# Where the split weights start inside their buffers, and a 64-byte shift of cross-attention operands, in a two-layer decoder on one core

## The chip, the core and the metric

The kernel runs on one core of one Trainium2 chip. The metric is device time in microseconds (us), the time from the launch's start to its end on the core. Three runs of the kernel before took 1091.21, 1092.42 and 1090.48 us; the median is 1091.21 us. Nothing runs on the other cores.

## The reference

The reference computes a decoder of two layers over 256 tokens of width 1024, in float32. Each layer adds three things to the residual x, each after an RMSNorm:

```python
for l in range(DEPTH):                       # DEPTH = 2
    h = rmsnorm(x, norm_mix[l])
    x = x + mixer_block(h, ...)              # z = h @ w_in; four token mixers; gates; w_branch; w_out
    x = x + cross_attention(rmsnorm(x, norm_xattn[l]), rmsnorm(mem, norm_mem[l]), wq, wk, wv, wo)
    x = x + squared_relu_mlp(rmsnorm(x, norm_mlp[l]), w_up, w_down)   # relu(h @ w_up)**2 @ w_down
return rmsnorm(x, norm_final)
```

In `mixer_block`, `w_in` has 6840 columns; 4096 of them are gates, the rest feed latent attention (MLA), a spatial gate, gated linear attention and a gated DeltaNet. Cross-attention has 4 heads of 256 over 256 memory tokens: scores are q times k, then a softmax, then its result times v. The hidden width of the MLP is 4096.

## The kernel before

**Two parts.** A float32 weight is not multiplied as it is. ScalarE (ACT) copies it, rounded, into a buffer `wh` of type float32r, and VectorE (DVE) writes the rest, `w - wh`, into `wl`. Activations are split the same way (`xh` and `xl`, `hh` and `hl`, and so on). Each product is then three matmuls, in `mm3`: high by high, high by low, low by high (L202 to L204).

**The stream of weights.** All weights lie in DRAM as a list of halves of [128, 1024] float32, 168 for each layer, in the order of use. `half()` (L178) takes the next one: every second call starts a transfer of 1 MB into one of three buffers `wr`, and each call splits one half into one of four buffers `wh` and one of four `wl`. A half holds eight blocks of 128 columns. In most products a block is the stationary operand (128 columns), and 256 columns of activations (all tokens) are the moving one; the profile writes such a matmul as `128*128 128x256`. In four places (`gemm_tok`) it is the other way round: 128 columns of activations are stationary and 512 columns of weights move.

**The stages of a layer**, in their order, with the number of halves: `z` (18, input columns), `tok` (4, by `gemm_tok`), MLA's two halves, `gate` (32), `k` (8), `br` (8, `w_branch`), `out` (8), `q` (8), `v` (8, by `gemm_tok`), `o` (8), `up` (32), `down` (32; by `gemm_tok` in the second layer). The many small products of the four mixers lie between the products of `gate`; the scheduler of the framework puts them there, by its own model of times. A gate product, a transpose or a sum of squares (L356, one column) that comes between two streamed products is called an interruption below.

**Places.** Each `wh` and `wl` buffer has 512 bytes of slack, and `PLACE` (L49) says for each stage at which byte the half begins, as a list of pairs (for `wh`, for `wl`) that successive halves take in turn: `b, c = (n // 4 for n in Stream.place[...])` (L189), then `wh[:, b : b + 1024]`. In the built program every `wh` and `wl` buffer starts at byte 256 modulo 512 of its partition, and the activations of the products with 256 columns (`xh`, `xl`, `hh`, `hl`, `mh`, `ml`, `ah`, `al`, `oh`, `ol`, `kx`, `qx`, `ph`, `pl`, `vx`, and so on) start at 448 modulo 512. Counted modulo 256, places 0 and 256 are therefore 64 bytes past the activations, places 128 and 384 are 192 bytes past them, and place 448 starts level with them. This text calls them **class A** (0, 256), **class B** (128, 384) and **class C** (448).

Before, by stage (place of `wh`, place of `wl`):

| stage | layer 0 | layer 1 |
|---|---|---|
| z | (0,0), (256,256): A | (256,256), (384,384): A and B by halves |
| gate | (256,256), (384,384): A and B by halves | (0,256): A |
| k | (0,0), (128,128): A and B by halves | (384,384), (0,0): B and A by halves |
| br | (128,128), (384,384): B | (0,0), (256,256): A |
| out, q, o | (256,256): A | (256,256): A |
| up | (256,384): A for `wh`, B for `wl` | (0,0), (256,256): A |
| down | 0, 128, 256, 384 in turn: A and B by halves | (448,448), `gemm_tok` |
| tok, MLA, v | (448,448): C | (448,448): C |

In cross-attention the scores (L1182) have q stationary and k moving, and the products with v (L1213) have v stationary and the softmax `ph`, `pl` moving; all four start at 448 modulo 512, so they are class C too.

Of the kernel before, what the change touches and what calls it, by code (L numbers as in the profile page):

```python
# [9 lines left out]
F32 = mybir.dt.float32  # L10
F32R = mybir.dt.float32r
# [32 lines left out]

SLACK = 512
ONE, TOK = [(256, 256)], [(448, 448)]
PLACE = [  # L49
    dict(z=[(0, 0), (256, 256)], tok=TOK, gate=[(256, 256), (384, 384)], k=[(0, 0), (128, 128)], br=[(128, 128), (384, 384)],  # L50
         out=ONE, q=ONE, v=TOK, o=ONE, up=[(256, 384)], down=[(0, 0), (128, 128), (256, 256), (384, 384)]),
    dict(z=[(256, 256), (384, 384)], tok=TOK, gate=[(0, 256)], k=[(384, 384), (0, 0)], br=[(0, 0), (256, 256)],
         out=ONE, q=ONE, v=TOK, o=ONE, up=[(0, 0), (256, 256)], down=TOK),
]
N_PIECE = 44
# [13 lines left out]
def decoder(ctx: ExitStack, tc: tile.TileContext, ws, xn_d, xt_d, mem_d, pos_d, fin_d, par_d, cst_d, msk_d, out_d):  # L69
# [12 lines left out]
    def nm(s):  # L82
        uid[0] += 1
        return f"{s}_{uid[0]}"
# [43 lines left out]
    xs += [cp.tile([P, 2, T], F32, name=f"x{j}") for j in range(1, 4)]  # L128
    hh, hl = [], []
    cs = cp.tile([P, T], F32, name="cs")  # L130
    rowm = cp.tile([P, T], F32, name="rowm")
# [41 lines left out]
    class Stream:  # L173
        i = 0
        raw = None
        place = PLACE[0]["z"]

    def half(parts=1):  # L178
        if Stream.i % 2 == 0:
            if Stream.i < 4:  # L180
                Stream.raw = raw0[Stream.i // 2]
            else:
                Stream.raw = wp.tile([P, 2048], F32, tag="wr", name=nm("wr"), bufs=3)
                nc.sync.dma_start(Stream.raw, ws[Stream.i // 2])
        o = 1024 * (Stream.i % 2)
        Stream.i += 1
        r = Stream.raw[:, o : o + 1024]
        wh, wl = (wp.tile([P, 1024 + SLACK // 4], F32R, tag=n, name=nm(n), bufs=4) for n in ("wh", "wl"))
        b, c = (n // 4 for n in Stream.place[Stream.i % len(Stream.place)])  # L189
        wh, wl = wh[:, b : b + 1024], wl[:, c : c + 1024]  # L190
        n = 1024 // parts
        for c in range(0, 1024, n):
            p = slice(c, c + n)
# [53 lines left out]
    def ch(tiles):  # L247
        return lambda k: tiles[k // 2][:, k % 2, :]
# [113 lines left out]

    def gate_tile(i, dt=F32, name="gt"):
        return ap.tile([P, 2, T], dt, tag=f"gt{i}", name=nm(name))

# [76 lines left out]
    def layer(l):  # L442
# [17 lines left out]

        def weights(stage):
            Stream.place = PLACE[l][stage]

        weights("z")


# [275 lines left out]
        def zin_rest():  # L742
# [13 lines left out]

            weights("tok")
            gemm_tok(X, XL, 8, ev_tok)

        def head_out(n, o, z, gcol, post, pre, name):  # L760
# [309 lines left out]
        if l == 0:  # L1070
            for j in range(4):
                for d, n in ((hh, "hh"), (hl, "hl")):
                    d.append(ap.tile([P, 2, T], F32R, tag=f"{n}{j}", name=nm(n)))
        for j in range(4):
# [52 lines left out]

        weights("gate")
        for m in range(8):
# [25 lines left out]
        weights("k")  # L1155
        gemm(ch(mh), ch(ml), 8, 4, ev_split(kh, kl, "kx"))

        weights("br")
        for m in range(8):
            merge(m)  # L1160
        rel(brh, brl)
        weights("out")

# [6 lines left out]
        qh, ql = [], []  # L1170
        weights("q")

        gemm(H, L, 8, 4, ev_split(qh, ql, "qx"), lead=True)
        px = [[None] * 2 for _ in range(2)]
        for a in range(2):
            for t in range(2):
# [11 lines left out]
                px[a][t] = p  # L1188
        rel(qh, ql, kh, kl)
        vh, vl = [[None] * 2, [None] * 2], [[None] * 2, [None] * 2]  # L1190
        weights("v")
        for nb in range(2):
            def ev_v(t, ps):
# [3 lines left out]
                vh[t][nb], vl[t][nb] = a, b  # L1197
            gemm_tok(ch(mh), ch(ml), 8, ev_v)
        rel(mh, ml)
        oh, ol = [], []  # L1200
        weights("o")
        for h in range(4):
            ps = bank()
            for mt in range(2):
                for t in range(2):
                    PE.transpose(ps[:, mt, 128 * t : 128 * t + 128], px[h // 2][t][:, h % 2, 128 * mt : 128 * mt + 128], ident)
            ph, pl = new(F32R, name="ph"), new(F32R, name="pl")
            split_ps(ph, pl, ps)
# [7 lines left out]
            oh.append(a), ol.append(b)  # L1216
            rel(ph, pl)
        rel(px, vh, vl)
# [21 lines left out]

        weights("up")
        gemm(H, L, 8, 16, ev_up, lead=True)
        weights("down")
        if l + 1 < NL:
# [6 lines left out]
    def final(rs, ah, al):  # L1251
# [16 lines left out]
        for nb in range(2):  # L1268

            @urgent  # L1270
            def evac(t, ps):
# [12 lines left out]
                S.dma_start(out_d[:, t, 512:1024], u)  # L1284

            gemm_tok(ch(ah), ch(al), 32, evac, 4 if nb else 1)
        rel(y, yg, gf, sq)
# [186 lines left out]
```

## Time and profile before

| | |
|---|---|
| median of three runs | 1091.21 us |
| the profiled execution | 1090.66 us |
| its span, from first to last instruction | 1088.3 us |
| TensorE matmul busy (PE) | 1064.5 us, 98% of the span |
| VectorE busy (DVE) | 812.7 us, 75% |
| ScalarE busy (ACT) | 583.8 us, 54% |
| matmuls in the trace | 8494 |

A matmul's record has a start and a modelled end, some 276 ns later. Matmuls are pipelined: the next one starts 113 to 118 ns after, while the first still runs. So the busy share and the duration say little of the pace; the pace is the distance from start to start. It is read here in two ways: in a list of instructions in order of time, from the column of starts, and in a table of stretches, from the count of matmuls in a stretch of known length.

### The profile page before, as it was taken

To read this page: it belongs to the slowest core of one execution; us is meant where nothing else is said; L and a number is where in the kernel's file an instruction comes from. 1 tells how busy PE (TensorE), PEld (TensorE's weight loads), DVE (VectorE), ACT (ScalarE), POOL (GpSimd) and SP (SyncE) were. 2 spreads that over 40 slices of the span, in tenths; PEclk is the share of its full clock that TensorE was granted. 3 is DMA by queue.
4 is the path that set the end of the run, shared out by engine and by line. 5 is a ranking of instruction groups with operands and counts; after the bars stand their busy time and mean duration, and the time that the engine had idled before them with its cause. 6 is when DMAs were issued, how large, how long until landed. Compare 5 with 4: busy or idle time off the path is not lost.

```text
span 1088.3 us, 20696 instructions
## 1 busy us (share of the span) xinstructions
PE 1064.5 (98%) x8494; PEld 1020.9 (94%) x8494; DVE 812.7 (75%) x1419; ACT 583.8 (54%) x875; POOL 197.6 (18%) x170
## 2 busy tenths in 40 slices
PE   9989999999999999999999999999999999999996
PEld 8979998899998999999999899989999899999885
DVE  7999857789866876655689997686797778665454
ACT  6565554554645666644455746544555555555342
POOL 6334005108300200000102321410451011010000
PEclk9999999999999999999999999999999999999998
DMA  9442523354544455555555343334455345554551
GB/s 364 170 173 107 207 105 122 112 194 156 194 155 155 160 195 195 194 194 194 195 188 202 140 167 141 117 144 152 171 193 194 132 142 192 194 206 165 194 191 39
DMA packets 28319, 185.13 MB, mean 170 GB/s; under 512 B 3392, under 2 KB 3648, under 8 KB 6976
## 3 DMA queue, kind: packets, MB, share of 16 engines
q1 hardware_dynamic: 26208, 179.09, 45.4%
q10 hardware_dynamic: 2016, 4.72, 1.3%
q8 instruction: 66, 1.08, 0.4%
q14 instruction: 29, 0.24, 0.1%
HBM read 182.75 MB, written 1.05 MB: 169 GB/s over the span
## 4 chain that ended last, share of the span: by engine, by line
PE 81%; DVE 11%; ACT 3%; DMA 2%; issue 1%; POOL 1%; ACTq 0%; DVEq 0%; POOLq 0%
PE g L202 24%; PE g L204 24%; PE g L203 24%; DVE wl L198 3%; DMA mr<-memt 2%; DVE qt L865 1%; PE ps L202 1%; ACT wh L195 1%; PE ps L203 1%; PE ps L204 1%; DVE gt L1116 1%; PE ps L666 1%; PE ps L670 1%; DMA wr<-ws 1%; DVE mgl L1124 1%
## 5 line engine op out<-in xcount | busy, mean ns | idle before, releaser
L198 DVE TENSOR_TENSOR wl<-wr,wh 128x1024 fp32r<-128x1024 f32 (+1 forms) x337 | 415.3, 1235 | 182.9 <-ACT wh L195 181.2
L195 ACT ACTIVATE wh<-wr 128x1024 fp32r<-128x1024 f32 (+1 forms) x337 | 355.1, 1057 | 332.9 <-PE g L203 233.8
L204 PE MATMUL g<-hh,wl 128*128 128x256 f32 x1152 | 324.0, 282 | 3.4 <-DVE wl L198 3.4
L202 PE MATMUL g<-hh,wh 128*128 128x256 f32 x1152 | 322.5, 281 | 1.9 <-ACT gt L1101 1.5
L203 PE MATMUL g<-hl,wh 128*128 128x256 f32 x1152 | 321.6, 279 | 0.0
L204 PEld LDWEIGHTS g<-hh,wl 128*128 128x128 f32 x1152 | 216.4, 188 | 5.6 <-DVE wl L198 4.4
L202 PEld LDWEIGHTS g<-hh,wh 128*128 128x128 f32 x1152 | 216.3, 188 | 3.1 <-ACT gt L1101 1.9
L203 PEld LDWEIGHTS g<-hl,wh 128*128 128x128 f32 x1152 | 218.0, 189 | 0.4 <-issue 0.2
L342 POOL TENSOR_TENSOR sq<-sq,sq 128x512 f32<-128x512 f32 x14 | 23.3, 1661 | 341.0 <-ACT sq L334 340.8
L203 PE MATMUL g<-xl,wh 128*128 128x256 f32 x272 | 75.4, 279 | 0.3 <-DVE xl L324 0.3
L202 PE MATMUL g<-xh,wh 128*128 128x256 f32 x272 | 74.8, 279 | 0.6 <-ACT xh L315 0.6
L204 PE MATMUL g<-xh,wl 128*128 128x256 f32 x272 | 74.5, 279 | 0.0
L202 PE MATMUL g<-ah,wh 128*128 128x256 f32 x256 | 70.7, 276 | 0.0
L203 PE MATMUL g<-al,wh 128*128 128x256 f32 x256 | 70.7, 276 | 0.0
L204 PE MATMUL g<-ah,wl 128*128 128x256 f32 x256 | 70.7, 276 | 0.0
L202 PEld LDWEIGHTS g<-xh,wh 128*128 128x128 f32 x272 | 50.8, 188 | 1.3 <-ACT xh L315 1.3
L1117 POOL TENSOR_TENSOR gt<-gt,gt 128x512 f32<-128x512 f32 x16 | 35.5, 2218 | 90.8 <-DVE gt L1116 89.9
L203 PEld LDWEIGHTS g<-xl,wh 128*128 128x128 f32 x272 | 51.1, 188 | 0.5 <-DVE xl L324 0.5
L204 PEld LDWEIGHTS g<-xh,wl 128*128 128x128 f32 x272 | 50.8, 189 | 0.0
L204 PE MATMUL g<-wh,al 128*128 128x512 f32 x128 | 49.5, 389 | 0.0
L203 PE MATMUL g<-wl,ah 128*128 128x512 f32 x128 | 49.5, 389 | 0.0
L202 PE MATMUL g<-wh,ah 128*128 128x512 f32 x128 | 49.4, 390 | 0.0
(500 smaller groups left out, 2331.0 us busy)
## 6 DMA issues: line engine op xcount, KB each, us to landing
wr<-ws SPq DMA_DIRECT2D x166, 1024.0 KB, 4.8
wr<-ws ACTq DMA_DIRECT2D x4, 512.0 KB, 7.5
mr<-memt ACTq DMA_DIRECT2D x8, 256.0 KB, 4.7
par<-par SPq DMA_DIRECT2D x2, 778.0 KB, 6.8
x<-xt SPq DMA_DIRECT2D x3, 256.0 KB, 7.8
cst<-cst SPq DMA_DIRECT2D x1, 588.0 KB, 8.4
gf<-fin SPq DMA_DIRECT2D x2, 256.0 KB, 5.3
yt<-yg ACTq DMA_DIRECT2D x2, 256.0 KB, 2.5
```

The costliest lines, as they stand in the source:

```text
L195: i = S.activation(wh[:, p], r[:, p], AF.Copy)
L198: V.tensor_tensor(wl[:, p], r[:, p], wh[:, p].bitcast(F32), op=ALU.subtract)
L202: PE.matmul(out, ah, bh, start=start, stop=False)
L203: PE.matmul(out, ah, bl, start=False, stop=False)
L204: PE.matmul(out, al, bh, start=False, stop=stop)
L342: G.tensor_tensor(acc, acc, sq, op=ALU.add)
L666: PE.matmul(xp[:, h], M[:, h], Tm[:, h], start=True, stop=True)
L670: PE.matmul(up[:, h], X[t][:, h], U[:, h], start=True, stop=True)
L865: V.tensor_tensor(qt[:, a].rearrange("p (b h) -> p b h", h=h), e3, halves(qbd[a // 2][:, a % 2], i)[:, :, 1], op=ALU.mult)
L1116: V.scalar_tensor_tensor(gt[m][a], gt[m][a], 1.0, ps, op0=ALU.add, op1=ALU.mult)
L1117: G.tensor_tensor(gt[m][0], gt[m][0], gt[m][1], op=ALU.add)
L1124: V.scalar_tensor_tensor(dl, t, 0.5, dh.bitcast(F32), op0=ALU.mult, op1=ALU.subtract)
```

## The change

The list `PLACE` goes. A half no longer lies in one piece: its first four blocks start at byte 256 of the buffer and its last four, shifted, at byte 2432 (`TURN`, in floats: 64 and 608). Modulo 512 of the partition the first four blocks start at 0 and the last four at 128: class A, then class B, in every half, in `wh` and in `wl` alike, in all stages with 256 moving columns and in MLA's two halves. `gemm_tok` keeps the address it had, 448 (`TOK`, in floats 112 and 624, without a gap). `wh` and `wl` are split with one instruction for a half as before; its shape is 2x512 in place of 1024. `Weights` translates a column of a half into its place.

q of cross-attention moves from the pool of general pieces into the tiles that the gates and `xh`, `xl` use, and `ph`, `pl` move into the tiles of `hh` and `hl`. These tiles are widened from 2048 to 2560 bytes, and in them q, `ph` and `pl` start 64 bytes later (`SHIFT`, 16 floats): at 0 modulo 512. k and v stay at 448.

On each of the five engines the instructions of the built program stand in the same order as before.

```diff
-SLACK = 512
-ONE, TOK = [(256, 256)], [(448, 448)]
-PLACE = [
-    dict(z=[(0, 0), (256, 256)], tok=TOK, gate=[(256, 256), (384, 384)], k=[(0, 0), (128, 128)], br=[(128, 128), (384, 384)],
-         out=ONE, q=ONE, v=TOK, o=ONE, up=[(256, 384)], down=[(0, 0), (128, 128), (256, 256), (384, 384)]),
...
-]
+W_BUF = 1152
+TURN, TOK = (64, 608), (112, 624)
+
+SHIFT = 16
...
+    class Weights:
+        def __init__(self, t, place):
+            self.t, self.place = t, place
+        def __getitem__(self, k):
+            c = k[1]
+            o = self.place[c.start // 512] - c.start // 512 * 512
+            return self.t[:, c.start + o : c.stop + o]
+
+    def two(t, place):
+        n = place[1] - place[0]
+        return t[:, place[0] : place[0] + 2 * n].rearrange("p (s c) -> p s c", s=2)[:, :, 0:512]
...
-        wh, wl = (wp.tile([P, 1024 + SLACK // 4], F32R, tag=n, name=nm(n), bufs=4) for n in ("wh", "wl"))
-        b, c = (n // 4 for n in Stream.place[Stream.i % len(Stream.place)])
-        wh, wl = wh[:, b : b + 1024], wl[:, c : c + 1024]
...
-                i = S.activation(wh[:, p], r[:, p], AF.Copy)
+                i = S.activation(hi, ri, AF.Copy)
...
-                V.tensor_tensor(wl[:, p], r[:, p], wh[:, p].bitcast(F32), op=ALU.subtract)
-        return wh, wl
+                V.tensor_tensor(lo, ri, hi.bitcast(F32), op=ALU.subtract)
+        return Weights(wh, Stream.place), Weights(wl, Stream.place)
...
+    def spaced(tag, dt, name, shift=0):
+        t = ap.tile([P, 640], dt, tag=tag, name=nm(name))
+        return t, t[:, shift : shift + 512].rearrange("p (a b) -> p a b", a=2)
...
-                a, b = new(F32R, name=name), new(F32R, name=name)
+                if name == "qx":
+                    a, b = (gate_tile(2 * p + i, F32R, name, SHIFT) for i in range(2))
+                else:
+                    a, b = new(F32R, name=name), new(F32R, name=name)
...
-            ph, pl = new(F32R, name="ph"), new(F32R, name="pl")
+            ph, pl = (hfull[2 * h + i][:, SHIFT : SHIFT + 512].rearrange("p (a b) -> p a b", a=2) for i in range(2))
```

## Rows read from the trace of the kernel before

**Rows 1.** The page: span; busy time and share of each engine; the chain of work that ended last, by engine.

```profile
span 1088.3 us, 20696 instructions
...
PE 1064.5 (98%) x8494; PEld 1020.9 (94%) x8494; DVE 812.7 (75%) x1419; ACT 583.8 (54%) x875; POOL 197.6 (18%) x170
...
PE 81%; DVE 11%; ACT 3%; DMA 2%; issue 1%; POOL 1%; ACTq 0%; DVEq 0%; POOLq 0%
```

**Rows 2.** Table of stretches: `up` of layer 0, `down` of layer 0 and `up` of layer 1, 80 us out of each. Columns: stretch in us from the span's start, its length, busy us and (x) number of instructions of each engine, granted TensorE clock, DMA share, GB/s.

```profile
375.00:455.00 80.00, 80.00 (x708) 80.00 (x707) 57.43 (x74) 49.07 (x61) 0.00 (x0) 1.00 0.54 197
462.00:542.00 80.00, 80.00 (x709) 80.00 (x708) 46.91 (x45) 35.77 (x41) 5.16 (x4) 1.00 0.54 197
906.00:986.00 80.00, 80.00 (x681) 80.00 (x681) 55.29 (x68) 46.95 (x59) 4.01 (x2) 1.00 0.54 196
```

**Rows 3.** The matmuls of TensorE in order of time at the start of `up` in layer 0, around the sum of squares (L356). Columns: start us, us, engine, line, operation, tiles, shapes, count.

```profile
374.81 0.28 PE L204 MATMUL g<-hh,wl 128*128 128x256 f32 x1
374.92 0.50 PE L356 MATMUL ps<-cst,sq 128*128 128x1 f32 x4
375.28 0.48 PE L202 MATMUL g<-hh,wh 128*128 128x256 f32 x2
375.60 0.28 PE L203 MATMUL g<-hl,wh 128*128 128x256 f32 x1
375.72 0.28 PE L204 MATMUL g<-hh,wl 128*128 128x256 f32 x1
375.84 0.28 PE L203 MATMUL g<-hl,wh 128*128 128x256 f32 x1
...
377.31 0.28 PE L204 MATMUL g<-hh,wl 128*128 128x256 f32 x1
```

**Rows 4.** The same list at the start of `up` in layer 1, around the same sum of squares.

```profile
903.98 0.28 PE L204 MATMUL g<-hh,wl 128*128 128x256 f32 x1
904.09 0.50 PE L356 MATMUL ps<-cst,sq 128*128 128x1 f32 x4
904.46 0.48 PE L202 MATMUL g<-hh,wh 128*128 128x256 f32 x2
904.77 0.28 PE L203 MATMUL g<-hl,wh 128*128 128x256 f32 x1
...
906.42 0.28 PE L203 MATMUL g<-hl,wh 128*128 128x256 f32 x1
```

**Rows 5.** The same list in `z` of layer 1: two transposes (L305) while a half of class B is used; the next half, of class A, begins with the row at 559.59.

```profile
558.67 0.38 PE L305 MATMUL ps<-cst,rsmixy 128*128 128x128 f32 x2
558.80 0.36 PE L202 MATMUL g<-xh,wh 128*128 128x256 f32 x1
559.00 0.28 PE L203 MATMUL g<-xl,wh 128*128 128x256 f32 x1
...
559.47 0.28 PE L204 MATMUL g<-xh,wl 128*128 128x256 f32 x1
559.59 0.28 PE L202 MATMUL g<-xh,wh 128*128 128x256 f32 x1
559.70 0.28 PE L203 MATMUL g<-xl,wh 128*128 128x256 f32 x1
559.83 0.28 PE L204 MATMUL g<-xh,wl 128*128 128x256 f32 x1
559.95 0.28 PE L202 MATMUL g<-xh,wh 128*128 128x256 f32 x1
560.06 0.28 PE L203 MATMUL g<-xl,wh 128*128 128x256 f32 x1
...
560.51 0.28 PE L204 MATMUL g<-xh,wl 128*128 128x256 f32 x1
```

**Rows 6.** The same list in `gate` of layer 0: a half of class B after an interruption; the next half, of class A, begins with the row at 145.62.

```profile
144.36 0.36 PE L204 MATMUL g<-hh,wl 128*128 128x256 f32 x1
...
145.62 0.28 PE L202 MATMUL g<-hh,wh 128*128 128x256 f32 x1
...
147.39 0.28 PE L202 MATMUL g<-hh,wh 128*128 128x256 f32 x1
```

**Rows 7.** Table of stretches (columns as in rows 2): `q` of layer 0 and of layer 1; two stretches of `k` in layer 1, before and after a half of class B is followed by one of class A.

```profile
296.00:310.00 14.00, 14.00 (x121) 14.00 (x120) 9.74 (x16) 7.05 (x11) 0.00 (x0) 1.00 0.51 188
825.00:839.00 14.00, 14.00 (x122) 14.00 (x121) 9.74 (x16) 7.05 (x11) 0.00 (x0) 1.00 0.50 191
...
763.00:766.00 3.00, 3.00 (x27) 3.00 (x27) 2.15 (x3) 1.95 (x3) 0.00 (x0) 1.00 0.10 22
...
770.00:773.00 3.00, 3.00 (x29) 3.00 (x29) 2.07 (x3) 1.06 (x1) 0.00 (x0) 1.00 0.52 175
```

**Rows 8.** Table of stretches: the end of `z` in layer 0 and in layer 1, then the whole of `gate` in layer 0 and in layer 1.

```profile
38.00:60.00 22.00, 21.99 (x186) 21.67 (x185) 21.85 (x40) 11.65 (x17) 4.39 (x3) 1.00 0.48 177
...
576.00:596.00 20.00, 20.00 (x173) 20.00 (x173) 20.00 (x32) 10.38 (x14) 4.52 (x3) 1.00 0.58 211
74.00:221.00 147.00, 139.69 (x1200) 133.88 (x1199) 118.07 (x305) 82.83 (x150) 40.54 (x41) 1.00 0.36 130
609.00:751.00 142.00, 139.06 (x1204) 134.02 (x1203) 110.40 (x287) 77.75 (x143) 31.84 (x35) 1.00 0.38 138
```

**Rows 9.** The list of matmuls at the first and the last pair of starts more than 115 ns apart in `gate` of layer 0 (419 of 763 starts).

```profile
75.25 0.28 PE L202 MATMUL g<-hh,wh 128*128 128x256 f32 x1
75.36 0.28 PE L203 MATMUL g<-hl,wh 128*128 128x256 f32 x1
...
220.81 0.28 PE L204 MATMUL g<-hh,wl 128*128 128x256 f32 x1
220.93 0.28 PE L202 MATMUL g<-mh,wh 128*128 128x256 f32 x1
```

**Rows 10.** Table of stretches, TensorE alone (columns: stretch, length, busy us and number of matmuls, granted clock, DMA share, GB/s): scores of cross-attention, and products with v, in layer 0.

```profile
312.70:316.70 4.00, 4.00 (x35) 1.00 0.37 107
347.20:350.20 3.00, 3.00 (x28) 1.00 0.00 0
```

**Rows 11.** Groups of DVE by line and shape, with the mean ns of one: the split of a half; a product of 512 contiguous elements; a product whose second operand is read as 2x256.

```profile
L198 DVE TENSOR_TENSOR wl<-wr,wh 128x1024 fp32r<-128x1024 f32 x335 | 414.0, 1238 | 176.4 <-ACT wh L195 174.7
...
L1237 DVE TENSOR_TENSOR al<-up,ah 128x512 fp32r<-128x512 f32 x32 | 22.1, 692 | 1.8 <-ACT ah L1236 1.7
...
L487 DVE TENSOR_TENSOR zc<-g,rrow 128x512 f32<-128x512 f32 x3 | 2.0, 680 | 0.0
```

More of the change, by code (lines that the diff above doesn't have):

```diff
@@ L43 @@
 PAD = 48
-SLACK = 512
-ONE, TOK = [(256, 256)], [(448, 448)]
-PLACE = [
-    dict(z=[(0, 0), (256, 256)], tok=TOK, gate=[(256, 256), (384, 384)], k=[(0, 0), (128, 128)], br=[(128, 128), (384, 384)],
-         out=ONE, q=ONE, v=TOK, o=ONE, up=[(256, 384)], down=[(0, 0), (128, 128), (256, 256), (384, 384)]),
-    dict(z=[(256, 256), (384, 384)], tok=TOK, gate=[(0, 256)], k=[(384, 384), (0, 0)], br=[(0, 0), (256, 256)],
-         out=ONE, q=ONE, v=TOK, o=ONE, up=[(0, 0), (256, 256)], down=TOK),
-]
+W_BUF = 1152
+TURN, TOK = (64, 608), (112, 624)
+SHIFT = 16
 N_PIECE = 44
@@ L129, in decoder @@
     hh, hl = [], []
+    hfull = []
     cs = cp.tile([P, T], F32, name="cs")
@@ L175, in decoder, with one @@
         raw = None
-        place = PLACE[0]["z"]
+        place = TURN
+    class Weights:
[5 more added lines that the diff above has]
+            return self.t[:, c.start + o : c.stop + o]
+    def one(t, place, c):
+        return t[:, place[c] : place[c] + 512]
+    def two(t, place):
+        n = place[1] - place[0]
+        return t[:, place[0] : place[0] + 2 * n].rearrange("p (s c) -> p s c", s=2)[:, :, 0:512]
     def half(parts=1):
@@ L187, in half @@
         r = Stream.raw[:, o : o + 1024]
-        wh, wl = (wp.tile([P, 1024 + SLACK // 4], F32R, tag=n, name=nm(n), bufs=4) for n in ("wh", "wl"))
-        b, c = (n // 4 for n in Stream.place[Stream.i % len(Stream.place)])
-        wh, wl = wh[:, b : b + 1024], wl[:, c : c + 1024]
-        n = 1024 // parts
-        for c in range(0, 1024, n):
-            p = slice(c, c + n)
+        wh, wl = (wp.tile([P, W_BUF], F32R, tag=n, name=nm(n), bufs=4) for n in ("wh", "wl"))
+        for c in range(parts):
+            ri, hi, lo = (two(t, p) if parts == 1 else one(t, p, c) for t, p in ((r, (0, 512)), (wh, Stream.place), (wl, Stream.place)))
             with tc.high_priority(offset=WP):
-                i = S.activation(wh[:, p], r[:, p], AF.Copy)
+                i = S.activation(hi, ri, AF.Copy)
                 if Stream.i <= 4:
                     tc.keep_in_program_order(i)
-                V.tensor_tensor(wl[:, p], r[:, p], wh[:, p].bitcast(F32), op=ALU.subtract)
-        return wh, wl
+                V.tensor_tensor(lo, ri, hi.bitcast(F32), op=ALU.subtract)
+        return Weights(wh, Stream.place), Weights(wl, Stream.place)
     def mm3(out, ah, al, bh, bl, start, stop):
@@ L361, in gain, with gate_tile @@
         return nrm[:, 8 * i : 8 * i + 8]
-    def gate_tile(i, dt=F32, name="gt"):
-        return ap.tile([P, 2, T], dt, tag=f"gt{i}", name=nm(name))
+    def spaced(tag, dt, name, shift=0):
+        t = ap.tile([P, 640], dt, tag=tag, name=nm(name))
+        return t, t[:, shift : shift + 512].rearrange("p (a b) -> p a b", a=2)
+    def gate_tile(i, dt=F32, name="gt", shift=0):
+        return spaced(f"gt{i}", dt, name, shift)[1]
     def operands(j, g, mix=False, parts=(slice(0, 2),), share=False):
@@ L459, in layer @@
         H, L = ch(hh), ch(hl)
-        def weights(stage):
-            Stream.place = PLACE[l][stage]
-        weights("z")
         zc = []
@@ L755, in ev_tok @@
                 R.zs.append(z)
-            weights("tok")
+            Stream.place = TOK
             gemm_tok(X, XL, 8, ev_tok)
+            Stream.place = TURN
         def head_out(n, o, z, gcol, post, pre, name):
@@ L1072, in layer @@
                 for d, n in ((hh, "hh"), (hl, "hl")):
-                    d.append(ap.tile([P, 2, T], F32R, tag=f"{n}{j}", name=nm(n)))
+                    t, v = spaced(f"{n}{j}", F32R, n)
+                    hfull.append(t), d.append(v)
         for j in range(4):
@@ L1126, in merge @@
                 rel(gt[m])
-        weights("gate")
         for m in range(8):
@@ L1161, in layer @@
         rel(brh, brl)
-        weights("out")
         gemm(ch(mgh), ch(mgl), 8, 4, residual(gain(4 * l + 1)), lead=True, tail=True)
@@ L1170, in layer @@
         qh, ql = [], []
-        weights("q")
         gemm(H, L, 8, 4, ev_split(qh, ql, "qx"), lead=True)
@@ L1188, in layer @@
                 px[a][t] = p
-        rel(qh, ql, kh, kl)
+        rel(kh, kl)
         vh, vl = [[None] * 2, [None] * 2], [[None] * 2, [None] * 2]
-        weights("v")
+        Stream.place = TOK
         for nb in range(2):
@@ L1198, in layer @@
             gemm_tok(ch(mh), ch(ml), 8, ev_v)
+        Stream.place = TURN
         rel(mh, ml)
         oh, ol = [], []
-        weights("o")
         for h in range(4):
@@ L1216, in layer @@
             oh.append(a), ol.append(b)
-            rel(ph, pl)
         rel(px, vh, vl)
@@ L1239, in ev_up @@
             rel(t)
-        weights("up")
         gemm(H, L, 8, 16, ev_up, lead=True)
-        weights("down")
         if l + 1 < NL:
@@ L1284, in evac @@
                 S.dma_start(out_d[:, t, 512:1024], u)
+            Stream.place = TOK
             gemm_tok(ch(ah), ch(al), 32, evac, 4 if nb else 1)
```

2 lines of the change are left out of this document (removed).

## The prediction

> **What bounds the kernel now.** I read the page first. TensorE is busy 98% of the span and carries 81% of the chain that ended last [rows 1], so TensorE's pace sets the end. A busy share near 100% does not show whether that pace is the best one, so the second view is the table of stretches, with a count of matmuls. In `up` of layer 0 and in `down` of layer 0, 80 us hold 708 and 709 matmuls; in `up` of layer 1, which runs the same code with other places, they hold 681 [rows 2]. Nothing waits in any of the three: PE is busy 80.00 of 80.00 us, the granted clock is 1.00, DVE and ACT have 20 us and more to spare. So there are two paces for one and the same matmul. 80 us over 708.5 is 112.9 ns, 80 us over 681 is 117.5 ns; the starts in the list of matmuls agree (375.84 to 377.31 us is 13 steps of 113 ns, 904.77 to 906.42 us is 14 steps of 118 ns) [rows 3, 4]. I call them close and wide; a wide one costs 4.5 ns more. Counted start to start over the whole trace, 2,604 of 6,560 streamed products with 256 columns are wide (116 to 126 ns), 3,955 close.
>
> The third view, the list in order of time, tells how the wide pace begins and ends. Both `up` stages are close until the sum of squares (L356) comes between two products. After it both are wide. In layer 0, where `wh` is in class A and `wl` in class B, the pace is close again from the fourth or fifth product on [rows 3]. In layer 1, where all lies in class A, it stays wide for the 30 halves that follow [rows 2, 4]. So an interruption sets the pace, and the places decide how long it lasts. To the starts I put the addresses of the built program and counted unbroken stretches in which one class is followed by the other while the pace is wide: from B to A it becomes close in 11 of 14 (one of them is close from the fourth product after the turn on [rows 5]), and stays wide in 3 (one of them [rows 6]); from A to B it becomes close in 0 of 9; from A to A (places 0 and 256) in 0 of 35. In 51 turns of either direction with a close pace it stayed close. Class C is always wide, 120 ns and more.
>
> **The change part by part.** *The turn inside each half.* Each half now goes A, B, and the next half begins with A: a turn from B to A after every 24 products in every stage, where before it came after 48 or never. A wide stretch should then last to the next half, or the one after, in place of to the end of its stage. I took each wide stretch of the trace and cut it at the first start of a half, with 8 cures in 10.
>
> - `up` of layer 1: 727 wide of 767, of which 12 are left; 715 x 4.5 ns = 3.2 us. DVE has 25 us of 80 to spare there [rows 2], so all of it reaches the end.
> - `q` in both layers: 152 wide of 192 each (14 us hold 121 and 122, while the close pace gives 126) [rows 2, 7]; some 17 are left: 2 x 135 x 4.5 ns = 1.2 us, passed on whole.
> - `k`: 55 and 109 wide, 48 left: 0.5 us; that a turn from B to A does it there is seen in 27 against 29 matmuls in 3 us [rows 7]. `out` of layer 1: 46 to 22, 0.1 us. `br`: 89 to 68, 0.1 us. MLA's products, class C before, 82 to 46: 0.15 us.
> - `gate`: 419 and 421 wide of 763 each (the first and the last of layer 0 in [rows 9]), cut to 306 and 207: 327 x 4.5 ns = 1.5 us. Here much is between the products and DVE is busy 118 of 147 and 110 of 142 us with the chains of the mixers [rows 8]; the chain goes over DVE for 11% of the span [rows 1]. I let half through: 0.7 us (bounds 0 and 1.5).
> - `z`: 336 wide, cut to 85: 1.1 us. But its wide products lie at its end, and there DVE is busy 21.85 of 22 and 20.00 of 20 us [rows 8]. A faster TensorE would only wait for `wl` (L198). I let 0.2 us through (bounds 0 and 1.1).
>
> `up` and `down` of layer 0 and `o` are close now and should stay so: nothing in 51 turns speaks for a loss. `gemm_tok` keeps its addresses: nothing.
>
> *The 64 bytes.* The scores run at class C: 35 matmuls in 4.00 us [rows 10], the edges taken off (33 steps) 121 ns. With q at 0 and k at 448 they become class A, so 113 to 118 ns; 95 products x 6.5 ns = 0.6 us at best, 0.25 us if they stay wide. For v at 448 stationary and the softmax at 0 moving, the trace has no row: the stationary is there 64 bytes before the moving operand modulo 256, no longer behind it. Its bounds are the level start it has now (28 in 3.00 us, some 115 to 121 ns) [rows 10], so 0, and the close pace, 90 x 7 ns = 0.6 us; a loss as large as the gain cannot be excluded either. I take 0.3 us. For the scores I take 0.6 us.
>
> *The splits.* 335 splits of a half are read and written as 2x512 in place of 1024. A product of DVE with an operand read as 2x256 took 680 ns, one with 512 contiguous elements 692 ns [rows 11]: no cost; at the worst a few ns on 1238, which DVE hides in `up` and which would cost 335 x 10 ns = 3 us only if it were on the chain everywhere, while the chain lies on DVE for 11%: 0.4 us. The order of instructions does not change on any engine, nor do SP's transfers; the widened tiles change addresses of other tiles by multiples of 512 only.
>
> *Sum.* 3.2 + 1.2 + 0.5 + 0.1 + 0.1 + 0.15 + 0.7 + 0.2 + 0.6 + 0.3 = 7.05, rounded 7 us. The profiled execution took 1090.66 us (span 1088.3 [rows 1] and 2.4 us around it), so it would be 1083.7; the median of the runs is 0.55 us above it, so the time is about 1084.2, said as 1084. The floor, all 2,604 close at once with both parts of cross-attention, is 2,604 x 4.5 ns + 1.2 = 12.9 us less: 1078.
>
> **The rivals.** *The turn cures less.* Twelve products of class B, not 24, come before each turn, and 3 of 14 turns failed; where the mixers interrupt every ten products a cure buys little. Then `up` and `q` still end close, since they have many halves to try, and the rest gives nothing: 1091.2 - 4.4 = 1087. Against it: five products of class B after the interruption were enough [rows 5].
>
> *Place does not set the pace.* What lies beside the interruption, the PSUM bank or the transfers, could decide, and the two `up` stages would differ by chance. Then the change does nothing that is measured: 1091. For it: close and wide are both found in each of classes A and B. Against it: the sums of squares [rows 3, 4] are the same code with the same neighbours, and 11 of 14 against 0 of 44 is no chance. The Trainium skill would have it so: its page "TensorE: Matmul & The Clock Gate", section "Back-to-back issue gap", makes the spacing a matter of the moving columns and the weight load alone (262 cycles at 256 columns) and knows no address. By that rule the time stays 1091. The trace disagrees with it: two paces for one form at one granted clock [rows 2].
>
> *Class B holds the wide pace, on the other side: slower.* An interruption in class A often heals by itself after one or two products; in class B I found none that healed before the next turn. Now half of all products of all stages are class B, also those of `up` and `down` in layer 0, which are close today. If the turn from A to B inside a half also starts a wide stretch, half of 6,560 products are wide, 676 more than now: 676 x 4.5 - 0.9 = 2.1 us slower, 1093.3; if the turn back does not cure, all are: 3,955 x 4.5 - 0.9 = 17 us slower, 1108. It decides from 40% wide products on (2,604 of 6,560). Against it: the 51 close turns, and `down` of layer 0, which goes through all four places at the close pace [rows 2].
>
> **How the numbers follow.** About what a measurement of this kernel can tell from no change is 0.2%, 2.2 us. I give the forecast (1079 to 1086) 0.67, the weaker cure (1086 to 1089) 0.14, no effect of place 0.11, the slower side 0.08. Faster by over 0.2% is the first two, 0.81; within 0.2% 0.11; slower 0.08. The range 1079.5 to 1089.5 holds the forecast and the weaker cure with all bounds of the unknown terms, but for the last 1.5 us towards the floor; it leaves out the last two cases, somewhat under 2 in 10.
>
> **What would show it.** In the changed kernel 80 us of `up` in layer 1 should hold 707 to 709 matmuls in place of 681, and both stages of layer 0 still 708; 14 us of `q` some 125. After the sum of squares the list should show wide starts up to the next half and close ones from there. The scores should hold 37 or 38 in 4 us in place of 35. The end of `z` should give the same time with idle gaps of TensorE before L198's buffers. DVE's split should still take about 1238 ns. I am wrong if `up` of layer 1 stays at 681, if the layer-0 stages fall below 700, or if `up` is close and the time has not moved.

## The result and the profile after

The changed kernel took 1083.87 us (median of 1083.77, 1083.87 and 1084.50), the kernel before 1091.21: 7.3 us less, a ratio of 0.9932 with a 95% interval of 0.9918 to 0.9946. The prediction was 1084.0, in a range of 1079.5 to 1089.5. The profiled execution took 1084.50 us with a span of 1082.7.

Line numbers are 11 higher than before in most places (L202 to L204 are L213 to L215, the split L198 is L209, the sum of squares L356 is L367). The page of the changed kernel, beside [rows 1] and the first of [rows 11]:

```profile
span 1082.7 us, 20698 instructions
...
PE 1058.8 (98%) x8494; PEld 1015.8 (94%) x8494; DVE 812.1 (75%) x1419; ACT 583.8 (54%) x875; POOL 196.3 (18%) x170
...
PE 81%; DVE 13%; ACT 2%; DMA 2%; issue 1%; POOL 0%; DVEq 0%; ACTq 0%
...
L209 DVE TENSOR_TENSOR wl<-wr,wh 128x1024 fp32r<-128x1024 f32 (+1 forms) x337 | 415.0, 1234 | 179.7 <-ACT wh L206 178.3
```

The busy shares tell nothing, as before: 98% of PE in both. The split costs 1234 ns with both its forms; on the page of before the same group had 1235, so the 2x512 shape is free. What moved shows in the table of stretches, the same three as [rows 2]:

```profile
375.00:455.00 80.00, 80.00 (x705) 80.00 (x706) 57.37 (x74) 48.99 (x61) 0.00 (x0) 1.00 0.54 197
462.00:542.00 80.00, 80.00 (x709) 80.00 (x708) 46.82 (x45) 35.70 (x41) 5.16 (x4) 1.00 0.55 198
906.00:986.00 80.00, 80.00 (x708) 80.00 (x708) 56.55 (x67) 47.88 (x59) 3.67 (x2) 1.00 0.57 204
```

`up` of layer 1 holds 708 matmuls in place of 681. `up` of layer 0 holds 705 in place of 708: a small loss. Why, the list of matmuls in `up` of layer 1 tells, beside [rows 4]:

```profile
901.49 0.28 PE L215 MATMUL g<-hh,wl 128*128 128x256 f32 x1
901.61 0.50 PE L367 MATMUL ps<-cst,sq 128*128 128x1 f32 x4
901.97 0.48 PE L213 MATMUL g<-hh,wh 128*128 128x256 f32 x2
902.29 0.28 PE L214 MATMUL g<-hl,wh 128*128 128x256 f32 x1
...
903.12 0.28 PE L213 MATMUL g<-hh,wh 128*128 128x256 f32 x1
...
905.95 0.28 PE L213 MATMUL g<-hh,wh 128*128 128x256 f32 x1
906.06 0.28 PE L214 MATMUL g<-hl,wh 128*128 128x256 f32 x1
...
907.99 0.28 PE L213 MATMUL g<-hh,wh 128*128 128x256 f32 x1
```

The sum of squares comes while the class B part of a half is used, and the pace is wide after it. By the addresses of the built program the next class A part begins with the row at 903.12. That turn cures nothing: up to 905.95 there are 24 steps of 118 ns. The class A part after it begins at 905.95, and from its first product on the pace is close: 906.06 to 907.99 is 17 steps of 113.5 ns. It stays close to the end of the stage. `up` of layer 0 and `q` of both layers do the same: the first turn after the sum of squares fails, the second cures, and some 32 products stay wide. In `up` of layer 0 a later interruption adds a shorter wide stretch; 51 products are wide there in all, where 5 were, and that is what it lost. Before, with `wh` in class A and `wl` in class B, four products were enough [rows 3].

The other stages gained too. Stretches of `q` (14 us, both layers), scores (4 us) and products with v (3 us), TensorE alone, beside [rows 7, 10]:

```profile
296.50:310.50 14.00, 14.00 (x125) 1.00 0.53 195
822.90:836.90 14.00, 14.00 (x125) 1.00 0.56 205
...
312.60:316.60 4.00, 4.00 (x38) 1.00 0.52 150
346.80:349.80 3.00, 3.00 (x28) 1.00 0.05 19
```

`q` holds 125 where it held 121 and 122, the scores 38 where they held 35. The products with v hold 28 as before. The end of `z` and the gates, both of layer 1, with all engines, beside [rows 8]:

```profile
576.00:596.00 20.00, 20.00 (x178) 20.00 (x177) 20.00 (x32) 10.66 (x14) 4.84 (x3) 1.00 0.59 211
609.00:751.00 142.00, 139.25 (x1214) 134.23 (x1215) 112.00 (x288) 78.41 (x143) 32.13 (x35) 1.00 0.38 138
```

The first holds 178 matmuls where it held 173, the second 1214 where it held 1204, with DVE as full as before. Over the whole trace 1,004 of 6,529 streamed products are wide, where 2,604 of 6,559 were.

One number would mislead: the profiled span is only 5.6 us shorter, the median time 7.3. In this execution the granted clock was 0.87 in the stretch from 7 to 20 us:

```profile
7.00:20.00 13.00, 12.18 (x90) 11.98 (x91) 12.28 (x15) 10.91 (x20) 10.19 (x7) 0.87 1.02 408
```

The matmul records there are 90, and `z` of layer 0 ended 0.9 us later than before. The mean hides two levels. From 8.7 to 12.0 us the granted clock stood at 0.50, the lower one (1.2 GHz; 1.00 is 2.4 GHz), and once more in `gate`, from 175.9 us on (TensorE alone):

```profile
8.70:12.00 3.30, 3.30 (x16) 0.50 1.06 425
...
175.90:179.20 3.30, 3.30 (x17) 0.50 0.69 231
```

Just ahead of the first of the two, TensorE had been idle for 1.44 us before its first product at 7.53 us; in the profile at full clock, in the last experiment, it was idle for 0.67 us there. Whether the change or that one execution does this is asked in the last experiment.

### The profile page after: what moved, and what is told of

Its sections match the earlier page's. It is cut to its first block, busy times and chain, and to the rows that moved or that the text cites. A ratio compares the mean times of both kernels' runs of the same rounds, so it can differ in the third digit from the quotient of the medians.

```text
span 1082.7 us, 20698 instructions
## 1 busy us (share of the span) xinstructions
PE 1058.8 (98%) x8494; PEld 1015.8 (94%) x8494; DVE 812.1 (75%) x1419; ACT 583.8 (54%) x875; POOL 196.3 (18%) x170
## 4 chain that ended last, share of the span: by engine, by line
PE 81%; DVE 13%; ACT 2%; DMA 2%; issue 1%; POOL 0%; DVEq 0%; ACTq 0%
PE g L214 24%; PE g L213 24%; PE g L215 24%; DVE wl L209 4%; DMA mr<-memt 2%; DVE qt L877 1%; PE ps L213 1%; PE ps L215 1%; PE ps L214 1%; DVE gt L1129 1%; ACT wh L206 1%; PE ps L677 1%; PE ps L681 1%; DVE cv L554 1%; DVE mgl L1137 1%
## 5 line engine op out<-in xcount | busy, mean ns | idle before, releaser
L209 DVE TENSOR_TENSOR wl<-wr,wh 128x1024 fp32r<-128x1024 f32 (+1 forms) x337 | 415.0, 1234 | 179.7 <-ACT wh L206 178.3
L215 PE MATMUL g<-hh,wl 128*128 128x256 f32 x1152 | 322.6, 280 | 3.6 <-DVE wl L209 3.6
L213 PE MATMUL g<-hh,wh 128*128 128x256 f32 x1152 | 321.1, 279 | 1.6 <-ACT gt L1114 1.1
L215 PEld LDWEIGHTS g<-hh,wl 128*128 128x128 f32 x1152 | 217.0, 188 | 6.0 <-DVE wl L209 4.8
L213 PEld LDWEIGHTS g<-hh,wh 128*128 128x128 f32 x1152 | 216.9, 189 | 2.8 <-ACT gt L1114 1.5
L213 PE MATMUL g<-xh,wh 128*128 128x256 f32 x272 | 74.8, 279 | 1.4 <-ACT xh L326 1.4
L215 PE MATMUL g<-xh,wl 128*128 128x256 f32 x272 | 74.7, 279 | 0.0
L213 PE MATMUL g<-ah,wh 128*128 128x256 f32 x256 | 70.7, 276 | 0.0
L215 PE MATMUL g<-ah,wl 128*128 128x256 f32 x256 | 70.7, 276 | 0.0
L213 PEld LDWEIGHTS g<-xh,wh 128*128 128x128 f32 x272 | 51.0, 189 | 1.8 <-ACT xh L326 1.8
L215 PEld LDWEIGHTS g<-xh,wl 128*128 128x128 f32 x272 | 51.2, 190 | 0.0
L215 PE MATMUL g<-wh,al 128*128 128x512 f32 x128 | 49.5, 389 | 0.0
L213 PE MATMUL g<-wh,ah 128*128 128x512 f32 x128 | 49.4, 390 | 0.0
```

The lines of the kernel that those rows point to most:

```text
L209: V.tensor_tensor(lo, ri, hi.bitcast(F32), op=ALU.subtract)
L213: PE.matmul(out, ah, bh, start=start, stop=False)
L215: PE.matmul(out, al, bh, start=False, stop=stop)
```

## The experiments

The theory: class A or B is the distance from the activations to the weights; an interruption can set the wide pace; a turn of the stationary operand from class B to class A brings the close one back; a close pace is not lost by a turn. Rivals: any turn does it; the operand's own address does it; place does nothing. Each kernel is compared with the kernel before on the same chip.

### One stage alone

The kernel before with one entry of its list changed, so that `up` of layer 1 has the places of layer 0:

```diff
-         out=ONE, q=ONE, v=TOK, o=ONE, up=[(0, 0), (256, 256)], down=TOK),
+         out=ONE, q=ONE, v=TOK, o=ONE, up=[(256, 384)], down=TOK),
```

> The kernel before, with one line of places changed: up of layer 1 gets (256,384), class A for wh and class B for wl, as up of layer 0 has it. If a turn from B to A cures the wide pace, 80 us of up in layer 1 hold 707 to 709 matmuls in place of 681, and the time falls by 3.2 us, to 1088.0. If the pace is not a matter of places, 681 and 1091.

Measured: 1087.94 against 1090.63, ratio 0.9974 (0.9965 to 0.9984). Its table of stretches, the third row of [rows 2]:

```profile
906.00:986.00 80.00, 80.00 (x708) 80.00 (x708) 57.20 (x75) 48.20 (x59) 3.66 (x3) 1.00 0.58 204
```

One entry of a list turns 681 into 708. Place sets the pace, and 2.7 us of the largest term, 3.2, show in the time (by the interval 1.7 to 3.8; by the trace `up` of layer 1 is 3.22 us shorter).

### All weights in one class

The changed kernel without its turn, all in class A; then all in class B:

```diff
-TURN, TOK = (64, 608), (112, 624)
+TURN, TOK = (64, 576), (112, 624)
```

> The changed kernel without the gap: every half in one piece at class A, no turn anywhere. If only the turn cures, up and down of layer 0 become wide too after the sum of squares (681 in 80 us in each), up of layer 1 and q as before the change: some 4,100 wide products, 1097 us. If both layers at equal places or the moved tiles were what helped, 1084; if places do nothing, 1091.

```diff
-TURN, TOK = (64, 608), (112, 624)
+TURN, TOK = (96, 608), (112, 624)
```

> The same with every half in one piece at class B. If class B never heals by itself, nearly every product with 256 columns is wide, 6,200 of 6,560: 1106 to 1107 us. If classes A and B are alike apart from the turn, as without the gap at class A, about 1097. If places do nothing, 1091.

Measured: class A 1097.46, ratio 1.0059 (1.0044 to 1.0074), 4,092 products wide; class B 1103.47, ratio 1.0112 (1.0095 to 1.0129), 6,333 wide. The three stretches of [rows 2] hold 682, 681 and 683 with class A, and 682, 682 and 681 with class B. The first of them with class A:

```profile
375.00:455.00 80.00, 80.00 (x682) 80.00 (x682) 54.96 (x72) 46.98 (x58) 0.00 (x0) 1.00 0.53 187
```

So without the turn the stages that were close in layer 0 are wide too, and class B holds the wide pace almost always. In class A some 2,450 products are close even so, since an interruption does not always bring the wide pace. Take the interruptions with at least six unbroken streamed products ahead and nine behind: with all in class A the wide pace follows in 20 of 39 cases when the pace ahead was close, and the close pace in 16 of 34 when it was wide. With all in class B a wide pace ended at 1 of 62. So some wide stretches end at an interruption and not at a turn.

The kernel all in class B is the world of the slower rival. It has 6,333 - 2,604 = 3,729 more wide products than the kernel before and is 12.8 us slower, 3.4 ns for each (a little more, since its scores are faster): most of the 4.5 ns reaches the end, not all.

### High parts in A, low parts in B

```diff
-TURN, TOK = (64, 608), (112, 624)
+TURN, TOK = (64, 576), (112, 624)
+LOW = (96, 608)
...
+        low = LOW if Stream.place is TURN else Stream.place
```

with `wl` split into `low` and read from there. A turn then comes in every group of three products.

> The changed kernel, with wh in one piece at class A and wl in one piece at class B: the turn from B to A comes with every third product in place of every 24th. If each such turn can cure, wide stretches last some four products, about 500 wide products in place of 1,200: 1081 us. If a turn cures only after a longer stay in class B, no cure: up and q wide as without any turn, 1095 or more.

Measured: 1081.94 against 1090.63, ratio 0.9920 (0.9904 to 0.9937), 516 products wide; the first two stretches hold 709 and 708. After the sum of squares in `up` of layer 1:

```profile
898.77 0.50 PE L369 MATMUL ps<-cst,sq 128*128 128x1 f32 x4
899.13 0.48 PE L215 MATMUL g<-hh,wh 128*128 128x256 f32 x2
...
899.69 0.28 PE L216 MATMUL g<-hl,wh 128*128 128x256 f32 x1
899.80 0.28 PE L217 MATMUL g<-hh,wl 128*128 128x256 f32 x1
...
902.29 0.28 PE L215 MATMUL g<-hh,wh 128*128 128x256 f32 x1
```

From 899.69 on the pace is close (23 steps in 2.60 us, 113 ns): it heals after four products, not 33. By medians the time is 1.9 us under the changed kernel's, but the intervals of the two ratios overlap.

### A turn within one class

The second four blocks lie 256 bytes away modulo 512 from the first, both in class A:

```diff
-TURN, TOK = (64, 608), (112, 624)
+TURN, TOK = (0, 576), (112, 624)
```

> The changed kernel with its two groups of four blocks 256 bytes apart in place of 128: both groups are class A, and the address still turns in every half. If the turn from B to A cures, and a turn as such does not, this is the kernel with everything in class A: 4,100 wide products, 681 matmuls in 80 us of up in both layers, 1097 us. If any jump of the address in mid-half cures: 1084.

Measured: 1098.06 against 1091.68, ratio 1.0057 (1.0042 to 1.0072); 682, 682 and 683 matmuls; 4,147 wide. As slow as all in class A: a jump of the address as such cures nothing. What counts is the place modulo 256.

### Weights and activations moved together

Both lie 64 bytes lower, so that the distance is kept and the address is not:

```diff
-PAD = 48
+PAD = 32
...
-TURN, TOK = (64, 608), (112, 624)
+TURN, TOK = (48, 592), (96, 608)
```

> The changed kernel with the activations and the weights both 64 bytes lower: their distance is kept, classes A and B as before, but all addresses modulo 256 are others. If the class is the distance between weights and activations: about 1,000 wide products, 1084. If the class is the weight's own address: its first blocks now stand where level weights stood, always wide at 120 ns, half of all products: 1105 or more.

Measured: 1084.36, ratio 0.9932 (0.9915 to 0.9948), 1,020 wide, stretches of 706, 708 and 708. The ratio of the changed kernel to the fourth digit: the classes are distances between the two operands, not addresses.

### The fourth distance

All weights 128 bytes past the activations modulo 256, called class D here:

```diff
-TURN, TOK = (64, 608), (112, 624)
+TURN, TOK = (16, 528), (112, 624)
```

> Every half in one piece at the class not seen so far, 128 bytes past the activations modulo 256 (class D), no turn. Level (class C) is always wide, 64 bytes away on either side (A and B) is wide for a time. If distance from the level place is what counts, D never stays wide: under 500 wide products, 1081. If D is sticky as A: 1097; as B: 1103.

Measured: 1109.77, ratio 1.0166 (1.0151 to 1.0181). No theory had it: the slowest of all kernels here. Its stretches hold 676, 676 and 671. The list in `down` of layer 0:

```profile
469.85 0.28 PE L215 MATMUL g<-ah,wl 128*128 128x256 f32 x1
...
470.80 0.28 PE L214 MATMUL g<-al,wh 128*128 128x256 f32 x1
...
472.11 0.28 PE L213 MATMUL g<-ah,wh 128*128 128x256 f32 x1
```

19 steps in 2.26 us, 119 ns on average. The steps of `down` lie between 115 and 122 ns, and none is at 113. The idea behind the expectation, that the distance from the level start decides, falls: level (class C) took 119.8 ns, 64 bytes away has a close and a wide pace, 128 bytes away (118.7 ns in `down`, 119.9 in `up` of layer 1) is about as bad as level.

### More turns in a half

Four pieces of six products in each half, in classes A, B, A, B, so that a turn from B to A comes after every 12 products in place of 24:

```diff
-TURN, TOK = (64, 608), (112, 624)
+TURN, TOK = (0, 288, 576, 864), (112, 624)
```

> The changed kernel with four groups of two blocks, 128 bytes further each, so A, B, A, B in each half: a turn from B to A after every 12 products in place of 24. If each turn cures with the same chance, wide stretches halve: some 600 wide products in place of 1,000, 1082. If a cure needs twelve products of class B, none: 1095 or more.

Measured: 1082.87, ratio 0.9922 (0.9907 to 0.9937), 767 wide; 706, 709 and 709. Twice the turns leave 237 fewer wide products than the changed kernel: fewer, as expected, but 767 and not the 600 of the expectation. Six products of class B before a turn are enough.

### The 64 bytes alone

The kernel before with the moved tiles and `SHIFT` of cross-attention; the list `PLACE` stays.

```diff
+SHIFT = 16
...
+                if name == "qx":
+                    a, b = (gate_tile(2 * p + i, F32R, name, SHIFT) for i in range(2))
```

> The kernel before with the 64-byte shift of cross-attention alone; all weights keep their old places. From the trace of the changed kernel the scores are 5.7 ns closer each (119.8 to 114.1 ns, 2 x 96 products, so 1.1 us for both layers at most) and the products with v 2.0 ns (119.8 to 117.8 ns, 0.4 us). The prediction's terms were 0.6 and 0.3 us. If they pass through whole, the time is 0.9 to 1.5 us under the kernel before, a ratio near 0.999; if the softmax and the splits around them set the end there, it is equal to the kernel before. The 4 us of the scores should hold 37 matmuls in place of 35, the 3 us of the products with v 28 as before or one more. up of layer 1 stays at 681 in 80 us.

Measured: 1090.01 against 1090.99, ratio 0.9992 (0.9984 to 1.0001): not to be told from no change. The expectation counted twice the products (there are 48 scores and 48 products with v in each layer), so it should have said 0.7 us. The trace has less still. The scores are at 117.8 ns, all 96 of them wide, while in the changed kernel they are at 114.1. Four microseconds of them, TensorE alone:

```profile
313.00:317.00 4.00, 4.00 (x36) 1.00 0.37 115
```

36 where the changed kernel has 38 and the kernel before 35. `q` just ahead of them is wide here (191 and 152 of 192), in class A like the scores, and without a turn the wide pace lasts. So most of the scores' gain is not the shift's alone. A close end of `q` is one way to it but not the only one. In the kernel with all weights in class D `q` is wide to its end, and the scores behind it, in class A, are close from the second one on (`q` and scores of layer 0 there, TensorE alone):

```profile
302.00:316.00 14.00, 14.00 (x119) 1.00 0.53 187
316.50:320.50 4.00, 4.00 (x38) 1.00 0.29 96
```

Behind a `q` all in class B the same scores stay wide, 117.8 ns in both layers.

From the start of `q` to the start of `v` this kernel is within 0.1 us of the kernel before in both layers, and the changed kernel 0.79 us shorter in each. A caution on such stretches: `out` of layer 0 is 0.64 us longer here, 148 wide against 2, at the same places. Which pace a stage finds at its start can differ between two kernels of equal placement.

The count of wide products does not give the time by itself. Some 3,110 are wide here, 500 more than before, and the time is not longer. In `gate` of layer 1 573 are wide against 425, and the stage takes the same time within 0.01 us; in `br` of both layers 329 against 89, and each is 0.06 us longer. In `out` of layer 0 the 146 more cost their 4.4 ns each.

### The mirror image

High parts in class B, low parts in class A:

```diff
-TURN, TOK = (64, 576), (112, 624)
-LOW = (96, 608)
+TURN, TOK = (96, 608), (112, 624)
+LOW = (64, 576)
```

> Mirror image of the kernel with the high parts in class A and the low parts in class B: here high parts in class B, low parts in class A, everywhere. Theory (a turn from B to A cures, the turn back does no harm): every group of three products has one such turn again (low to high was B to A before, now high to low), so the same time as its mirror image, 1082 us, and wide starts about as rare (500 to 700). Rival (what counts is how many products are in class A): two thirds are now class B in place of one third, and with all in B at 1103 and all in A at 1097 the time lies above its mirror image, 1085 or more.

Measured: 1101.17 against 1090.99, ratio 1.0092 (1.0078 to 1.0106), 4,274 wide. The theory's 1082 falls by 19 us. The list after the same sum of squares:

```profile
913.85 0.50 PE L369 MATMUL ps<-cst,sq 128*128 128x1 f32 x4
914.21 0.48 PE L215 MATMUL g<-hh,wh 128*128 128x256 f32 x2
914.53 0.28 PE L216 MATMUL g<-hl,wh 128*128 128x256 f32 x1
...
915.97 0.28 PE L217 MATMUL g<-hh,wl 128*128 128x256 f32 x1
```

12 steps in 1.44 us, 120 ns; the kernel with the classes the other way round was close from 0.9 us after this point. All of `down` in layer 0 runs so (675 in 80 us), with a turn from B to A in each of its 256 groups of three, and none cures. A turn to class A that is followed by one product of A and then by B again does not do it; two products of A in a row do it (high parts in A), and so do 6 and 12. Part of the theory stands: a close pace is not lost here either (`up` of layer 1 is close until the sum of squares). The rival that counts class A products has the sign, but not the size: none in A gives 1103, a third 1101, half 1083 to 1084, two thirds 1082, all 1097. The scores of this kernel, all in class A, are close from the first one on in both layers, right behind a wide `q`; that speaks for the run of A products, but it is two cases. Whether the number of class A products in a row is the cause, or which of the three products has which class, was not separated.

### A version with the softmax in class A

High parts in A, low parts in B, and the softmax parts 64 bytes below v:

```diff
-            ph, pl = (hfull[2 * h + i][:, SHIFT : SHIFT + 512].rearrange("p (a b) -> p a b", a=2) for i in range(2))
+            ph, pl = (hfull[2 * h + i][:, 112:624].rearrange("p (a b) -> p a b", a=2) for i in range(2))
```

> The kernel with high parts in class A and low parts in class B, and besides it the softmax parts of cross-attention put 64 bytes below v modulo 512 (class A) in place of 64 bytes above it. Theory: the products with v go from 117.8 ns to the 113 to 114 ns of the scores, 192 products in both layers x 4 ns = 0.8 us at most, so 1081.2 to 1081.9 against 1081.9 for the same kernel without this step; the 3 us of the products with v should hold 29 or 30 in place of 28. Rival: what holds them at 118 ns is not the place, and both count and time stay.

Measured: 1083.07, ratio 0.9924 (0.9910 to 0.9937): faster than the kernel before, and not to be told from the same kernel without this step (0.9920). The step works where it is made: of 92 steps between products with v 36 are wide in place of 92, and from the start of `o` to that of `up` the time is 0.12 us shorter in each layer. (The expectation again counted twice the products; 0.4 us was the most.) What hides it is larger: gates and `z`, where nothing differs between the two kernels, took 2.4 us more in this profiled execution (half a microsecond of it in `z` of layer 0, where the granted clock began at 0.87 again). So 0.25 us cannot be seen in the times.

### The changed kernel again

> The changed kernel again, unchanged, on the same chip as the three others: 1083.9 us, 7.3 us under the kernel before, whichever theory holds. In its first profiled execution the granted clock was 0.87 in the first 20 us, and its span was only 5.6 us shorter than that of the kernel before. If that low clock is what hid the rest, a profiled execution at full clock there is about 7 us shorter in span and the first stage does not lose its 0.9 us; if the stage z of layer 0 itself became slower by the change, it is late by 0.9 us again at clock 1.00.

Measured: 1083.55 against 1090.99, ratio 0.9931 (0.9918 to 0.9943). The stretch from 7 to 20 us:

```profile
7.00:20.00 13.00, 12.31 (x106) 12.11 (x107) 12.31 (x15) 12.54 (x21) 10.16 (x7) 1.00 1.02 407
```

At a clock of 1.00 the stretch has 106 matmuls, the span is 1081.7, 6.6 us under that of before, and `z` of layer 0 is 0.24 us shorter than before, not 0.8 longer. So the late start in the first profile was that execution's clock, not the change.

## Why the prediction was right

The total was right (7.05 us forecast, 7.3 and 7.4 by medians), and the mechanism as far as it was put to use. The terms can be compared stage by stage, from the start of a stage's first product to that of the next stage's, in the second profile of the changed kernel, whose first stretch ran at full clock like that of before:

| term | forecast, us | measured, us |
|---|---|---|
| `up` of layer 1 | 3.2 | 3.08 |
| `q` and the scores, both layers | 1.2 + 0.6 | 2 x 0.79 = 1.58 |
| `k` | 0.5 | 0.26 (all in layer 1) |
| `gate` with MLA | 0.7 + 0.15 | 1.30 |
| `z` | 0.2 | 0.73 |
| `br`, `out` | 0.2 | -0.13 |
| `o` with the products with v | 0.3 | 0.09 |
| `up` of layer 0 | 0 | -0.20 |
| `tok` of layer 0, the rest | 0 | -0.12 |
| sum | 7.05 | 6.60 |

The sum agrees with the span (6.6). The times differ by some tenths more, because what lies around the span is not fixed: 2.4 us in the profiled execution of before, 1.8 and 1.7 in those of the changed kernel, 1.7 to 2.8 in the experiments.

*Right.* That TensorE's pace, not its busy share, bounds the kernel; that `up` of layer 1 would hold 707 to 709; that the scores would hold 37 or 38; that the split's shape costs nothing; that close stretches survive turns: none of 385 turns at a close pace lost it. The cure came in 30 of 40 turns from B to A; I had put 8 in 10, from 11 of 14. None of 20 turns from A to B with a wide pace ended it.

*Too low: `z` and the gates.* The step "A faster TensorE would only wait for `wl`" failed. In layer 1, where nothing else disturbs the comparison, `z` became 0.49 us shorter in both profiles with DVE busy 20.00 of 20 us as before [rows 8]. It has 105 fewer wide products; at 4.5 ns each that is 0.47 us, so there the term went through whole. A full DVE in a stretch is not yet the bound: the products still ran back to back (PE 20.00 of 20.00), and the forecast idle gaps before L198's buffers did not come. Why DVE kept up is not shown; its work of the mixers may not all lie ahead of the next split. For the gates "I let half through" was the estimate, 0.85 us with MLA, and 1.30 came. That term is soft: between the two profiles of the changed kernel the gates of one layer differ by 0.1 to 0.3 us, and between two experiments with equal code there by 0.9. Since 148 more wide products in `gate` of layer 1 cost nothing in the experiment with the 64 bytes alone, it is argued and not shown that fewer wide products made the 1.30.

*Too high: products with v.* With the stationary operand 64 bytes before the moving one they run at 118.0 ns, 91 of 92 steps wide; before, level, 119.7. That is 0.2 us in all, and 0.09 is what the stage shows. The step that failed is "the trace has no row": 64 bytes before is 192 bytes past modulo 256, so by the text's own count it is class B, for which there were rows, and wide ones [rows 7]. At the wide pace of class B, 117.8 ns in the kernel all in B, the term is 0.2 us, not 0.3. The experiment with the softmax on the other side, in class A, gets about as much again. The bounds (0 and 0.6) held it.

*Missed: small losses.* "`up` and `down` of layer 0 and `o` are close now and should stay so" holds for `down` (768 of 768 close) but not for `up`: the interruption comes whatever the placement, and the first turn after it failed there; some 50 products wide, 0.20 us. The 51 turns were of stretches that are close; I did not ask how fast the old placement healed compared with the new. Small losses of this kind are also in `k` of layer 0 (65 wide against 55), `out` of layer 0 (20 against 2) and `br` of layer 1 (47 against 14). In time `k` of layer 0, `br` and `out` together lose 0.17 us. The 0.15 us in `tok` of layer 0 I can't place.

*The rivals.* "Place does not set the pace" is refuted by kernels with the same instructions at other places, from 1081.94 to 1109.77 us, and by one entry of a list (1087.94). With it falls the rule of the Trainium skill's page "TensorE: Matmul & The Clock Gate", section "Back-to-back issue gap", by which the spacing is the same in all of them: the measured steps are 113 and 118 ns, and 119 to 120 in other distances. The 262 cycles that the prediction took from it the Trainium skill gives in that section for the isolated gap, without the weight load. "The turn cures less" did not happen as a whole, though one in four fails. The slower rival is real where its condition is met, in the kernels of one class: 1103.47 where it was put at 1108, since a wide product costs 3.4 ns at the end, not 4.5. In the changed kernel 15% are wide, far from the 40% at which it decides.

*Right by luck, in part.* The account was a turn from B to A. The mirror image shows that the turn is not enough by itself. In the changed kernel 12 products of A follow each turn, so that the difference did not matter. Nor is class B needed ahead of them: the scores became close behind class D too.

What stays open: why the distance modulo 256 bytes between the stationary and the moving operand sets two paces, why an interruption can bring the wide one, and why one turn in four fails. No run here shows more than that it does.

## What to carry to other kernels

When one engine is busy 98% of the time, count its instructions in equal stretches of stages that should be alike: 681 against 708 in 80 us was the whole finding, and no busy share showed it. A pace that an event sets and that then lasts is priced by how long it lasts, so try small changes of operand placement on one stage, and read the list just behind the interruption. Where a gain falls in a stretch in which another engine is full, look whether the first engine has any gap there before writing the gain off; and take a second profile before explaining a microsecond that only one execution shows.

## What was not expected

- The distance of 128 bytes modulo 256 is the worst: 1109.77 us, steps of 119 ns in `down`, 671 to 676 matmuls in 80 us.
- High parts in A and low parts in B give 1081.94 us, the other way round 1101.17: 19 us between two kernels that differ in which of two buffers starts 128 bytes later.
- With the high parts in class A and the low parts in class B the pace heals after four products behind the sum of squares, with A and B in pieces of 12 after 33, since the first turn fails in `up` of both layers and in `q`.
- The granted clock from 7 to 20 us was 0.87 in some profiled executions and 1.00 in others of the same kernel, with 3.3 us of the stretch at 0.50, worth up to 1 us of `z` in layer 0.
